# Feed-forward chunks of a decoder trunk grouped 2,2,2,1,2,2 in place of 2,2,2,2,1,2, with three groups in place of two going down in seven products

## The chip, the cores and the metric

The kernel runs on one core of one Trainium2 chip. The time is that of the device in microseconds (us) from launch to end; the lower the better. Engines are called as in the profile: PE (TensorE matmul), PEld (its weight loads), DVE (VectorE), ACT (ScalarE), SP (SyncE, which issues nearly all DMAs here), POOL (GpSimd).

## The reference

Input x is 512 tokens by 1024 channels in float32. There are two layers; each is a feed-forward block, a mixer (gated linear attention in the first layer, stick-breaking attention in the second) and another feed-forward block, all on a residual stream. So there are four feed-forward blocks, called FFN 1 to FFN 4 here:

```python
def swiglu(h, w_gate, w_up, w_down):
    return (jax.nn.silu(h @ w_gate) * (h @ w_up)) @ w_down

x = x + 0.5 * swiglu(rmsnorm(x, ffn1_norm[i]), ffn1_w_gate[i], ffn1_w_up[i], ffn1_w_down[i])
...
x = x + 0.5 * swiglu(rmsnorm(x, ffn2_norm[i]), ffn2_w_gate[i], ffn2_w_up[i], ffn2_w_down[i])
```

w_gate and w_up are 1024 by 2816, w_down is 2816 by 1024. The change touches only how these three products are cut.

## The kernel before, in words

**Number format.** Every float32 matrix is split into a high part and the remainder (names ending in h and l: `wh`, `wl` of a weight, `hh`, `hl` of the hidden activations). A product is three matmuls: high by high, low by high, high by low. The split of a loaded weight (`raw` or `rawd`) is one cast on ACT (line L527, writes `wh`) and one subtraction on DVE (line L528, writes `wl`).

**Chunks.** The 2816 hidden channels are cut into 11 chunks of 256. A chunk has a gate product, an up product (each 1024 by 256 weights), and then its 256 rows of w_down. Chunks 2 to 10 take gate and up in seven half-size products in place of eight (Strassen-Winograd, method `seven`): sums of weight quarters are made on DVE (L1082, L1083, L1088, L1089), seven products of 12 matmuls each run over 256 tokens (L1097, tiles `ps_w`, `ps_q`, `ps_z`), and results are combined on ACT and DVE. For one chunk the gate is 84 matmuls, the up 84.

**Groups and the way down.** Chunks are gathered in groups. Going down, a group of two chunks is a product of 512 hidden channels by 1024 outputs. Its usual form (function `down`) is four parts of 24 matmuls over 512 tokens, `ps_d` at L469, each with one 128x1024 weight tile to split and two additions into the residual tiles (L727). The other form (function `seven_down`) is two parts; a part loads two 512 KB blocks (`lower`, `upper`, both tagged `rawd`, of which there are two buffers in all), makes four sums on DVE (L756, L757, L763, L764), takes seven products of 12 matmuls over 256 tokens (L772) and does twelve half-size additions into the residual (L778). A group that goes down this way must close its activations differently as well (`close_first`, `close_second`): four subtractions at L1265 and more splits at L1195 for every chunk.

In the list of work a group's way down stands inside the next group: between its gates and ups. The last group's stands at the end.

**What sets the order.** The program is written as a list of entries (`feed`), and a planner in the kernel (class `Planner`) then sets the order of each engine's instructions by a list schedule with prices of its own: 148 + 1.045 n for a DVE operation of n columns, 2000 ns + bytes / 400 for a DMA. PE, DVE, ACT and SP then run in exactly that order; each waits at its own front for what the instruction there needs. Eight PSUM banks are handed out in turn; a part of `seven_down` holds five, a gate or up in seven products three. Split weights have four buffers, loaded gate and up weights two.

The lines that matter here are the tables of the class FFN and the two places where the parts of `seven_down` are put into the list:

```python
GROUPS = ((0, 2), (2, 4), (4, 6), (6, 8), (8, 9), (9, 11))
DOWN_SEVEN = (1, 3)
...
if late and i == late[0][0]:
    seven_down(*late.pop()[1])
...
if group - 1 in self.DOWN_SEVEN and i == 1:
    args = (lambda: self.tp, wd, self.GROUPS[group - 1][0] * 256, self.hs[group - 1])
    seven_down(*args, 0)
    late.append((0 if slots > 2 else 1, (*args, 1)))
```

Of the kernel before, what the change touches and what calls it, by code (L numbers as in the profile page):

```python
# [435 lines left out]
def decoder(ctx: ExitStack, tc: tile.TileContext, a: dict, out: bass.AP):  # L436
# [43 lines left out]
    class Chunk:  # L480
        def __init__(self, src, n, m):
            self.src, self.n, self.m, self.t = src, n, m, None
            self.pool = None
            self.few = False
# [95 lines left out]
    feed = Feed()  # L580

    def cols(w, c0, n):
        return w[:, c0 : c0 + n].rearrange("(k p) c -> p k c", p=P)

    def feat(ch, f, evac, tag=None, defer=None):


        def body(W):
            (wh, wl), = W
            ps = psum("ps_f", tag)  # L590
            for part in (range(u, u + KD // 4) for u in range(0, KD, KD // 4)):
                for k in part:
                    mm3(ps, wh[:, k], wl[:, k], st["h"][k], st["l"][k], k == 0, k == KD - 1)
                if part[-1] == KD - 1:
                    if defer is None:
                        evac(ps)
                    else:
                        defer.append((evac, ps))
                yield

        feed.q.append(Entry([(ch, lambda t: t[:, :, f * P : (f + 1) * P], KD, P)], body))
        feed.q[-1].evac = evac
# [97 lines left out]
    def down(w, r0, nf, hs, part, nxt, late=0):  # L700


        nd = KD // nf
        src = w[r0 : r0 + nf * P, part * nd * P : (part + 1) * nd * P]
        ch = Chunk(src.rearrange("(f p) c -> p f c", p=P), nf, nd * P)
        ch.few = True

        def body(W):
            (wh, wl), = W
            acc = []  # L710

            def prod(m, fs):
                if m == len(acc):
                    acc.append(psum("ps_d"))
                s = slice(m * P, (m + 1) * P)
                for f in fs:
                    mm3(acc[m], wh[:, f, s], wl[:, f, s], hs[f][0], hs[f][1], f == 0, f == nf - 1)

            if late:
                for m in range(nd):  # L720
                    prod(m, range(nf - late))
            for m in range(nd):
                prod(m, range(nf - late if late else 0, nf))
                ps = acc[m]
                k = part * nd + m
                x = pair(xs[k])
                nc.vector.scalar_tensor_tensor(  # L727
                    out=x, in0=flat(ps), scalar=0.5, in1=x, op0=ALU.mult, op1=ALU.add
                )
                if nxt is not None:  # L730
                    nxt(k)
                yield

        feed.q.append(Entry([(ch, lambda t: t, nf, nd * P)], body))
# [99 lines left out]
    def back_tok(w, r0, nf, hs, done):  # L834


        units = []
        for dh in range(2):
            src = w[r0 : r0 + nf * P, dh * 512 : dh * 512 + 512]
            ch = Chunk(src.rearrange("(f p) c -> p f c", p=P), nf, 512)  # L840
            for u in range(0, nf, 2):
                units.append((ch, (lambda t, u=u: t[:, u : u + 2]), 2, 512))

        def body(W):
            for i in range(NT):
                s = slice(i * P, (i + 1) * P)
                for dh in range(2):
                    cuts = (0, 256, 512) if (i, dh) == (NT - 1, 1) else (0, 512)
                    for c0, c1 in zip(cuts, cuts[1:]):
                        ps = psum("ps_bt")[:, 0 : c1 - c0]  # L850
                        c = slice(c0, c1)
                        for f in range(nf):
                            wh, wl = W[dh * (nf // 2) + f // 2]
                            hh, hl = hs[f]
                            mh, ml = turns(wh[:, f % 2, c]), turns(wl[:, f % 2, c])
                            mm(ps, hh[:, s], mh, f == 0, False)
                            mm(ps, hh[:, s], ml, False, False)
                            mm(ps, hl[:, s], mh, False, f == nf - 1)
                        done(dh, i, ps, c0, c1)
            yield  # L860

        feed.q.append(Entry(units, body))
# [132 lines left out]
    class FFN:  # L995
# [3 lines left out]

        GROUPS = ((0, 2), (2, 4), (4, 6), (6, 8), (8, 9), (9, 11))
        NORMED, SEVEN, AHEAD = 6, 2, 2
        DOWN_SEVEN = (1, 3)
        SEVEN_UP = (2, 3, 4, 5, 6, 7, 8, 9, 10)

        def __init__(self, wg, wu, wd, gi, nxt, first=False, last=False):
            self.gi, self.normed = gi, False
            self.after_ffn = bool(phases) and isinstance(phases[-1], FFN)
            self.defer, self.gates = [], []  # L1010
            self.lead = []
            self.hs = [[] for _ in self.GROUPS]
            base, downs, late = len(feed.q), [], []
            self.sums_by = 10**6
            for group, (c0, c1) in enumerate(self.GROUPS):
                slots, put = 2 * (c1 - c0), 0
                if group == 1:

                    for put in range(self.AHEAD):
                        down(*downs[put], late=put == 0)  # L1020
                    put = self.AHEAD
                for i in range(slots):
                    c, f = c0 + i // 2, i % 2
                    if f == 0:
                        g, u = Chunk(cols(wg, c * 256, 256), KD, 256), Chunk(cols(wu, c * 256, 256), KD, 256)
                    d = self.defer if i == 0 and c == 0 else None
                    f_ = f
                    if first and c == 0:

                        g, u = (Chunk(cols(w, f * P, P), KD, P) for w in (wg, wu))  # L1030
                        self.lead += [g, u]
                        f_ = 0
                    if c >= self.SEVEN:
                        if f == 0:
                            self.sums_by = min(self.sums_by, len(feed.q) - base)
                            self.seven(g)
                    elif c not in self.SEVEN_UP:
                        feat(g, f_, self.evac_g, defer=d)
                    elif f == 0:
                        feat(g, 0, self.evac_g), feat(g, 1, self.evac_g)  # L1040
                        self.sums_by = min(self.sums_by, len(feed.q) - base)
                    if c not in self.SEVEN_UP:
                        feat(u, f_, lambda ps, h=group: self.evac_u(ps, h), defer=d)
                    elif f == 1:
                        self.seven(u, group)

                    if late and i == late[0][0]:
                        seven_down(*late.pop()[1])
                    while c >= self.SEVEN and put < len(downs) * (i + 1) // slots:
                        down(*downs[put])  # L1050
                        put += 1
                    if group - 1 in self.DOWN_SEVEN and i == 1:
                        args = (lambda: self.tp, wd, self.GROUPS[group - 1][0] * 256, self.hs[group - 1])
                        seven_down(*args, 0)

                        late.append((0 if slots > 2 else 1, (*args, 1)))
                for x in downs[put:]:
                    down(*x)
                n = 2 * (c1 - c0)
                end = group + 1 == len(self.GROUPS)  # L1060
                downs = [(wd, c0 * 256, n, self.hs[group], part, nxt if end else None) for part in range(n)]
                if group in self.DOWN_SEVEN:
                    downs = []
            self.count = len(feed.q) - base
            if last:
                back_tok(wd, c0 * 256, n, self.hs[group], nxt)
            else:
                for x in downs:
                    down(*x)
            self.total = len(feed.q) - base  # L1070

        def seven(self, ch, group=None):
# [89 lines left out]
            def close_0(o0):  # L1162
                if group in self.DOWN_SEVEN:
                    self.close_first(o0, group)
                else:
                    self.close(o0, group)

            def close_1(o0, o1):
                if group in self.DOWN_SEVEN:
                    self.close_second(o0, o1, group)  # L1170
                else:
                    self.close(o1, group)
# [1116 lines left out]
```

## Time and profile before

| | us |
|---|---|
| median of 3 runs | 1762.15 |
| lowest, highest | 1761.73, 1762.88 |
| the profiled execution's own time | 1761.07 |
| its span, first to last instruction | 1759.3 |
| PE busy | 1748.0 (99%) |
| DVE busy | 1530.7 (87%) |
| ACT busy | 1055.2 (60%) |
| DMA, mean | 102 GB/s |

An engine's busy time is the time in which at least one of its instructions is running. Durations of single instructions overlap the next one's start on PE, ACT and DVE, so what an instruction costs its engine is the distance from its start to the start of the next when nothing is waited for. The granted PE clock was 0.999 over the span.

### The profile page before, as it was taken

The page shows a single profiled execution, that of the slowest core. Times are in us where ns is not written, and L with a number is a line of the kernel's source. Part 1 is how long each engine was busy: PE and PEld are TensorE (multiplying, and loading weights), DVE is VectorE, ACT ScalarE, POOL GpSimd, SP SyncE. Part 2 cuts the span into 40 slices and gives each one's busy share as a digit, 9 for nine tenths or more (in the row PEclk, how much of TensorE's full clock was granted, in tenths as well). Part 3 has the DMA queues.
Part 4 walks back from the last instruction along what each step waited for, and adds up shares of the span by engine and source line. Part 5 has one row for each costly group of instructions (what it writes and reads, how often), then busy time and mean ns, then how long its engine had stood idle before and what let it go on. Part 6 is the DMA issues. An engine that isn't in the chain of part 4 may idle for free.

```text
span 1759.3 us, 31137 instructions
## 1 busy us (share of the span) xinstructions
PE 1748.0 (99%) x12714; PEld 1631.7 (93%) x12714; DVE 1530.7 (87%) x2516; ACT 1055.2 (60%) x1830; POOL 9.9 (1%) x24
## 2 busy tenths in 40 slices
PE   9999999999999999999999999999999999999998
PEld 8999999899888899999889999999888889999997
DVE  8998898787888999988799988986898679999986
ACT  7556565545656566555556655656889755665554
POOL 0000000100000000000000000000000000000000
PEclk9999999999999999999999999999999999999999
DMA  6334323421233331432424343332222233324331
GB/s 192 120 97 133 108 73 110 142 73 50 72 96 96 120 110 60 147 117 85 148 72 129 97 131 110 108 97 72 61 73 73 72 96 120 121 68 148 97 130 50
DMA packets 178755, 179.24 MB, mean 102 GB/s; under 512 B 4082, under 2 KB 170276, under 8 KB 178612
## 3 DMA queue, kind: packets, MB, share of 16 engines
q1 hardware_dynamic: 177760, 175.91, 31.8%
q8 instruction: 99, 1.62, 0.4%
q0 software_dynamic: 608, 1.05, 0.2%
q14 instruction: 44, 0.36, 0.1%
q10 hardware_dynamic: 244, 0.29, 0.0%
HBM read 175.17 MB, written 2.10 MB: 101 GB/s over the span
## 4 chain that ended last, share of the span: by engine, by line
PE 87%; DVE 7%; DMA 2%; ACT 2%; issue 1%; SPq 0%; DVEq 0%; ACTq 0%
PE ps_w L1097 21%; PE ps_d L469 15%; PE ps_f L469 13%; PE ps_q L1097 11%; PE ps_z L1097 5%; PE ps_t L469 5%; PE ps_w L772 4%; PE ps_b L469 3%; PE ps_q L772 2%; DVE wl L528 2%; DMA raw<-in_ffn_w_gate_dram 1%; PE ps_z L1777 1%; PE ps_z L772 1%; DMA raw<-in_ffn_w_up_dram 1%; PE ps_S L469 1%
## 5 line engine op out<-in xcount | busy, mean ns | idle before, releaser
L528 DVE TENSOR_TENSOR wl<-raw,wh 128x1024 fp32r<-128x1024 f32 x241 | 254.4, 1058 | 50.1 <-ACT wh L527 49.2
L527 ACT CAST wh<-raw 128x1024 fp32r<-128x1024 f32 x241 | 221.6, 921 | 114.0 <-PE ps_f L469 26.3
L527 ACT CAST wh<-s 128x1024 fp32r<-128x1024 f32 x176 | 184.1, 1047 | 98.7 <-DVE s L1083 21.3
L1097 PE MATMUL ps_w<-th,wh 128*128 128x256 f32 x864 | 237.6, 275 | 0.0
L1097 PE MATMUL ps_w<-tl,wh 128*128 128x256 f32 x864 | 237.6, 275 | 0.0
L1097 PE MATMUL ps_w<-th,wl 128*128 128x256 f32 x864 | 237.6, 275 | 0.0
L528 DVE TENSOR_TENSOR wl<-s,wh 128x1024 fp32r<-128x1024 f32 x176 | 213.3, 1217 | 10.1 <-ACT wh L527 9.8
L469 PE MATMUL ps_f<-xh,wh 128*128 128x512 f32 x432 | 166.4, 385 | 0.0
L1097 PEld LDWEIGHTS ps_w<-th,wl 128*128 128x128 f32 x864 | 165.9, 192 | 0.0
L1097 PEld LDWEIGHTS ps_w<-th,wh 128*128 128x128 f32 x864 | 165.9, 192 | 0.0
L1097 PEld LDWEIGHTS ps_w<-tl,wh 128*128 128x128 f32 x864 | 165.9, 192 | 0.0
L469 PE MATMUL ps_f<-xh,wl 128*128 128x512 f32 x432 | 163.7, 379 | 0.0
L469 PE MATMUL ps_f<-xl,wh 128*128 128x512 f32 x432 | 163.7, 379 | 0.0
L469 PE MATMUL ps_d<-hh,wh 128*128 128x512 f32 x416 | 158.8, 382 | 0.8 <-ACT wh L527 0.7
L469 PE MATMUL ps_d<-hl,wh 128*128 128x512 f32 x416 | 157.9, 380 | 0.9 <-DVE hl L1195 0.9
L469 PE MATMUL ps_d<-hh,wl 128*128 128x512 f32 x416 | 157.7, 379 | 0.0
L527 ACT CAST wh<-rawd 128x1024 fp32r<-128x1024 f32 (+1 forms) x100 | 82.9, 846 | 73.6 <-PE ps_d L469 62.7
L528 DVE TENSOR_TENSOR wl<-rawd,wh 128x1024 fp32r<-128x1024 f32 (+1 forms) x100 | 94.9, 962 | 14.2 <-ACT wh L527 13.4
L469 PEld LDWEIGHTS ps_f<-xl,wh 128*128 128x128 f32 x432 | 81.6, 189 | 11.5
L469 PEld LDWEIGHTS ps_f<-xh,wh 128*128 128x128 f32 x432 | 81.7, 189 | 11.0
L469 PEld LDWEIGHTS ps_f<-xh,wl 128*128 128x128 f32 x432 | 81.7, 189 | 10.7
L469 PEld LDWEIGHTS ps_d<-hl,wh 128*128 128x128 f32 x416 | 78.7, 189 | 12.5 <-DVE hl L1195 1.8
(349 smaller groups left out, 5236.9 us busy)
## 6 DMA issues: line engine op xcount, KB each, us to landing
raw<-in_ffn_w_gate_dram SPq DMA_DIRECT2D x43, 1024.0 KB, 5.4
raw<-in_ffn_w_up_dram SPq DMA_DIRECT2D x43, 1024.0 KB, 5.5
rawd<-in_ffn_w_down_dram SPq DMA_DIRECT2D x84, 512.0 KB, 6.5
raw<-in_gla_w_in_dram SPq DMA_DIRECT2D x12, 1024.0 KB, 5.3
raw<-in_sb_w_in_dram SPq DMA_DIRECT2D x16, 512.0 KB, 3.7
raw<-in_gla_w_out_dram SPq DMA_DIRECT2D x4, 1024.0 KB, 5.0
raw<-in_sb_w_in_dram SPq DMA_DIRECT2D x4, 1024.0 KB, 5.0
raw<-in_sb_w_out_dram SPq DMA_DIRECT2D x4, 1024.0 KB, 5.2
```

What stands on the lines that cost most here:

```text
L469: nc.tensor.matmul(ps, l, r, start=first, stop=last)
L527: nc.scalar.copy(h[:, k], part)
L528: nc.vector.tensor_tensor(out=l[:, k], in0=part, in1=h[:, k].bitcast(F32), op=ALU.subtract)
L772: st["pe"] = nc.tensor.matmul(ps, l_, r_, start=first and c + n == 0, stop=c == 1 and n == 2, skip_group_check=True).ins
L1097: st["pe"] = nc.tensor.matmul(o, l_, r_, start=first and j + n == 0, stop=j == 3 and n == 2, skip_group_check=True).ins
L1777: nc.tensor.matmul(o_, l_, r_, start=first, stop=last, skip_group_check=True)
```

## The change

The groups become 2,2,2,1,2,2 chunks: the group of one chunk is now the fourth and not the fifth. Groups 1, 2 and 4 go down in seven products in place of groups 1 and 3 (groups are counted from 0; each of these has two chunks). Both parts of a `seven_down` now stand in the list behind the first gate of the next group and before that chunk's up; before, part 0 stood behind the first up of that group and part 1 later, behind another chunk's gate or up.

```diff
-        GROUPS = ((0, 2), (2, 4), (4, 6), (6, 8), (8, 9), (9, 11))
+        GROUPS = ((0, 2), (2, 4), (4, 6), (6, 7), (7, 9), (9, 11))
         NORMED, SEVEN, AHEAD = 6, 2, 2
-        DOWN_SEVEN = (1, 3)
+        DOWN_SEVEN = (1, 2, 4)
...
                     elif f == 0:
                         feat(g, 0, self.evac_g), feat(g, 1, self.evac_g)
                         self.sums_by = min(self.sums_by, len(feed.q) - base)
+                    if group - 1 in self.DOWN_SEVEN and f == 0 and c == c0:
+                        args = (lambda: self.tp, wd, self.GROUPS[group - 1][0] * 256, self.hs[group - 1])
+                        seven_down(*args, 0)
+                        seven_down(*args, 1)
...
-                    if late and i == late[0][0]:
-                        seven_down(*late.pop()[1])
...
-                    if group - 1 in self.DOWN_SEVEN and i == 1:
-                        args = (lambda: self.tp, wd, self.GROUPS[group - 1][0] * 256, self.hs[group - 1])
-                        seven_down(*args, 0)
-
-                        late.append((0 if slots > 2 else 1, (*args, 1)))
```

Lines behind the table move up by three (L1097 becomes L1094, L1195 becomes L1192).

The planner sets a new order. The first place is SP's queue in FFN 3, from the last usual load of group 0's way down on. `rawd` are blocks of w_down, `raw` weights of a gate or an up. Before:

```order
L494 DMA rawd_11202<-in_ffn1_w_down_dram 128x4x256
L494 DMA rawd_11308<-in_ffn1_w_down_dram 128x4x256
L494 DMA raw_11313<-in_ffn1_w_gate_dram 128x8x256
L494 DMA raw_11439<-in_ffn1_w_up_dram 128x8x256
L494 DMA raw_11575<-in_ffn1_w_gate_dram 128x8x256
L494 DMA rawd_11701<-in_ffn1_w_down_dram 128x4x256
L494 DMA rawd_11822<-in_ffn1_w_down_dram 128x4x256
L494 DMA rawd_11827<-in_ffn1_w_down_dram 128x4x256
L494 DMA raw_11883<-in_ffn1_w_up_dram 128x8x256
```

Now:

```order
L494 DMA rawd_11209<-in_ffn1_w_down_dram 128x4x256
L494 DMA raw_11283<-in_ffn1_w_gate_dram 128x8x256
L494 DMA rawd_11367<-in_ffn1_w_down_dram 128x4x256
L494 DMA rawd_11507<-in_ffn1_w_down_dram 128x4x256
L494 DMA rawd_11512<-in_ffn1_w_down_dram 128x4x256
L494 DMA rawd_11620<-in_ffn1_w_down_dram 128x4x256
L494 DMA raw_11625<-in_ffn1_w_up_dram 128x8x256
L494 DMA raw_11755<-in_ffn1_w_gate_dram 128x8x256
L494 DMA raw_11885<-in_ffn1_w_up_dram 128x8x256
```

Before, three loads of gate and up weights stood between part 0's two blocks (11202, 11308) and part 1's (11701, 11822). Now part 1's blocks (11512, 11620) follow part 0's (11367, 11507) directly; since there are two `rawd` buffers, each is issued when DVE has read the block two loads ahead of it for the last time.

The second place is DVE at the passage from part 0's preparation to part 1's in that pair, now:

```order
L528 TENSOR_TENSOR wl_11611<-rawd_11367,wh_11610 128x512
L528 TENSOR_TENSOR wl_11611<-rawd_11507,wh_11610 128x512
L1192 TENSOR_TENSOR t34_11500<-ts_11486,t34_11499 128x512
L1140 TENSOR_TENSOR o1_11549<-u3_11639,o1_11549 128x256
L1144 TENSOR_TENSOR o0_11548<-ps_q_11546,o0_11548 128x256
L528 TENSOR_TENSOR wl_11617<-s34_11542,wh_11616 128x1024
L756 TENSOR_TENSOR s12_11622<-rawd_11620 128x512
L763 TENSOR_TENSOR s34_11670<-rawd_11512,rawd_11620 128x512
L757 TENSOR_TENSOR s12_11622<-s12_11622,rawd_11512 128x512
```

The first two rows are the last readers of part 0's blocks; the row of L756 is the first of part 1's. Four DVE instructions stand between them. In the order before, 38 stood there.

More of the change, by code (lines that the diff above doesn't have):

```diff
@@ L1012, in __init__ @@
             self.hs = [[] for _ in self.GROUPS]
-            base, downs, late = len(feed.q), [], []
+            base, downs = len(feed.q), []
             self.sums_by = 10**6
```

## The prediction

> **What bounds the kernel now.** I read the page's busy table first, then the groups by line, then the chain of waits and the timeline around one pass of `seven_down`. The busy table and the biggest wait of PE in the feed-forward blocks:
>
> ```profile
> PE 1748.0 (99%) x12714; PEld 1631.7 (93%) x12714; DVE 1530.7 (87%) x2516; ACT 1055.2 (60%) x1830; POOL 9.9 (1%) x24
> L469 PE MATMUL ps_d<-hh,wh 128*128 128x512 f32 x416 | 158.8, 382 | 0.8 <-ACT wh L527 0.7
> ```
>
> PE works all the time, so its matmul time is what a change can win. DVE is second, and its 87% is a mean. By stretches it looks like this: the first row is FFN 1 from the first way down to the last up, the second the same of FFN 3, the third two gates and ups with a part of `seven_down` in FFN 3 between them.
>
> ```profile
> 52.30:305.80 253.50, 253.50 (x2065) 247.51 (x2065) 232.73 (x383) 146.08 (x257) 1.04 (x1) 1.00 0.34 107
> 917.60:1166.20 248.60, 248.49 (x2042) 242.96 (x2042) 225.86 (x372) 142.41 (x251) 0.00 (x0) 1.00 0.34 108
> 1085.43:1123.15 37.72, 37.72 (x339) 37.72 (x338) 37.24 (x64) 23.95 (x44) 0.00 (x0) 1.00 0.20 64
> ```
>
> Columns: stretch and length, then busy time (instructions) of PE, PEld, DVE, ACT, POOL, then PE clock, DMA share, GB/s. Over the body DVE is idle for about 21 of 250 us; around `seven_down` it is idle for 0.5 of 37.7 us, and PE still does not wait. So DVE may be full for a while without harm: it runs ahead of PE. How far shows in the timeline, at the start of that part:
>
> ```profile
> 1097.68 0.69 DVE L528 TENSOR_TENSOR wl<-rawd,wh 128x512 fp32r<-128x512 f32 x1
> ...
> 1104.30 0.28 PE L772 MATMUL ps_w<-nh,wl 128*128 128x256 f32 x1
> ```
>
> The weight that PE takes at 1104.30 was split by 1097.68 + 0.69 = 1098.37, a lead of 5.9 us.
>
> **The change part by part.** *PE.* One group per FFN goes from the usual form to seven products. Both rates stand in the chain of waits:
>
> ```profile
> 1051.29 5.18 PE ps_d L469 x24
> 1104.35 1.34 PE ps_w L772 x12
> ```
>
> Usual form: 4 parts of 24 matmuls are 4 x 5.18 = 20.72 us. Seven products: 2 parts x 7 x 12 matmuls are 14 x 1.34 = 18.76 us. That is -1.96 us for each FFN, -7.84 us in all.
>
> *DVE.* What an operation costs there is the distance between starts, read where nothing waits:
>
> ```profile
> 1105.91 1.21 DVE L528 TENSOR_TENSOR wl<-s,wh 128x1024 fp32r<-128x1024 f32 x1
> 1107.04 0.68 DVE L528 TENSOR_TENSOR wl<-raw,wh 128x512 fp32r<-128x512 f32 x1
> 1107.64 0.41 DVE L778 SCALAR_TENSOR_TENSOR x<-ps_q,x 128x256 f32<-128x256 f32 x1
> 1107.98 0.41 DVE L778 SCALAR_TENSOR_TENSOR x<-ps_w,x 128x256 f32<-128x256 f32 x1
> ```
>
> 1.13 us for 1024 columns (1105.91 to 1107.04), 0.60 for 512 (to 1107.64), 0.335 for 256. The usual way down: 4 splits of 1024 and 8 additions of 512, 4.5 + 4.8 = 9.3 us. `seven_down`: 8 sums of 512, splits of 6 x 512 and 4 x 1024, 24 additions of 256: 4.8 + 3.6 + 4.5 + 8.0 = 20.9 us, which is more than its 18.8 us of PE. Closing the group's activations costs 8 subtractions of 256 (2.7 us) and splits of 4 x 256 and 5 x 512 in place of 4 x 512 (4.3 against 2.4 us). So DVE gets 11.6 + 2.7 + 1.9 = 16.2 us more for each FFN while PE gets 2.0 less.
>
> Does it fit? By groups, as DVE / PE us. A gate is 7.1 / 9.4; an up 9.6 / 9.4, or 11.95 / 9.4 where the group closes for seven products; the single chunk's way down 7.1 / 10.4 (2 splits, 8 additions). Before, the groups 2 to 5 with the way down that stands in each: 54.3/56.3, 47.4/58.2, 37.6/37.5, 40.5/47.9. Now: 59.0/56.3, 37.6/37.5, 45.2/47.9, 54.3/56.3. Sums: 179.8/199.9 before, 196.1/198.0 now. DVE's free time there shrinks from 20 us to 1.9 us, but it still fits, and only the first of the four groups is now clearly over PE, by 2.7 us, less than the lead of 5.9.
>
> *Inside a pair.* The two parts now follow each other, so I count along the orders of DVE and PE in FFN 3 from the first split of part 0 (lead 5.9) to the split or addition whose product comes tightest. Pair 1 (in group 2): 19.3 us of DVE against 15.4 of PE leaves 2.0. Pair 2: 15.0 against 10.6 leaves 1.6. Pair 3: 15.7 against 10.6 leaves 0.9. None goes under zero: DVE's work alone makes no stall.
>
> *The loads.* Part 1's two blocks are loaded into the buffers of part 0 when DVE has read them for the last time. The DVE work in the order between the last reader of part 0's second block and the first reader of part 1's is 2.4, 4.35 and 3.1 us in the pairs 1, 2, 3 of each FFN, the same in all four. How long a load takes: a pair of issues, 0.6 us apart, then the time to landing (last column) of its first and its second, of a block issued alone, and the page's median:
>
> ```profile
> 1100.80 0.97 SPq L494 DMA_DIRECT2D rawd<-in_ffn_w_down_dram  x2
> ...
> rawd<-in_ffn_w_down_dram SPq DMA_DIRECT2D x1, 512.0 KB, 3.6
> ...
> rawd<-in_ffn_w_down_dram SPq DMA_DIRECT2D x1, 512.0 KB, 5.0
> ...
> rawd<-in_ffn_w_down_dram SPq DMA_DIRECT2D x1, 512.0 KB, 3.4
> ...
> rawd<-in_ffn_w_down_dram SPq DMA_DIRECT2D x84, 512.0 KB, 6.5
> ```
>
> A second block issued 0.6 us behind a first takes 5.0; one with the queue to itself 3.5. In pair 1 the two buffers come free 0.6 us apart, so I take 5.0: DVE stands for 5.0 - 2.4 = 2.6 us at L756, and behind that instruction stand the additions into the residual that PE needs before it may go on in `ps_w`; 2.6 against a margin of 2.0 is a stall of 0.6 us. In the pairs 2 and 3 they come free 1.8 us apart, so I take 3.6: no wait in pair 2, and 0.5 against 0.9 in pair 3. That is +0.6 us for each FFN, +2.4 in all. Bounds: with 3.4 everywhere nothing stalls; with the median of 6.5 everywhere it is 2.1 + 0.5 + 2.5 = 5.1 us for each FFN, +20.4 in all. The median comes from blocks queued behind 1024 KB loads of gates and ups, and here the queue in front is empty of these, so I stay near the single issues.
>
> *The PSUM banks.* A pair takes ten banks of eight. Part 1's first `ps_q` product takes the bank of part 0's second `ps_w`, whose last addition it must wait for; PE has 1.34 us of other work between. One addition is 0.41 us; behind one split of 1.21 it is 1.6. So between nothing and 0.3 us a pair; I take nothing, since the margins above already count that addition.
>
> *The end of an FFN.* The single chunk's way down no longer stands between the last up and the last group's way down, so the closing of the last chunk has less cover. It is a multiplication, a cast and a split in a row:
>
> ```profile
> L1110 DVE TENSOR_TENSOR o<-o,o 128x256 f32<-128x256 f32 x72 | 30.4, 422 | 1.8
> L1194 ACT CAST hh<-o 128x512 fp32r<-128x512 f32 x56 | 34.8, 621 | 6.0 <-DVE o L1110 5.8
> L1195 DVE TENSOR_TENSOR hl<-o,hh 128x512 fp32r<-128x512 f32 x56 | 37.4, 682 | 0.0
> ```
>
> Their means make 1.7 us, covered by the 9 matmuls that can go first, 9 x 5.18 / 24 = 1.9 us. Bounds 0 and, if DVE is as late as it allowed itself with 5.18 us more in front, some 2 us; I take 0.2 for FFN 1 to 3, +0.6; in FFN 4 the 32 transposes still stand between. In return the 0.7 us that `ps_d` waited for ACT's cast goes, since that product is moved into the block.
>
> The sum: 1761.07 - 7.84 + 2.4 + 0.6 - 0.7 = 1755.5 us in terms of the profiled execution, whose span is 1759.3. The median of the runs is 1.1 above that execution, so I forecast 1756.6 us.
>
> **The rivals.** *All of it is kept.* No load is late: 1761.07 - 7.84 - 0.7 = 1752.5, with the 1.1 1753.6 us. For it speaks that PE had next to no waits before, with DVE as full as in the third stretch; against it that DVE has 1.9 us free where it had 20.
>
> *DVE becomes the bound and the gain is given back.* DVE cannot use every nanosecond: in 1085.43:1123.15, with work at hand all the time, it is idle 1.3% of the time, in the body as a whole 8 to 9%, for want of work or behind ACT's casts. If 5% of the 196.1 us are lost to such waits, the groups 2 to 5 need 205.9 on DVE against 198.0 of PE; 5.9 of that lies in the lead at the start, and the other 2.0 us for each FFN are all that it wins: 1762 us, no change.
>
> *The loads are late in every pair.* This is the one that ends slower. Its place is DVE's front at the first sum of part 1, its price is landing time less the 2.4, 4.35 or 3.1 us of work in between, less the margin. It decides from a landing of 5.2 us in the pairs 1 and 3 (0.8 + 1.2 = 2.0 us, all that an FFN wins); at 6.5 the time is 1762.15 - 7.84 + 20.4 = 1774.7 us. Against it stands that nothing is queued in front of these blocks.
>
> *Every DVE operation costs its whole length.* Then a gate is 7.9, an up 10.95 or 13.8, the pair 24.4 and the groups 2 to 5 now 224.4 us on DVE against 198.0: about 26 - 6 = 20 us for each FFN, some 1835 us. The rows above with starts 0.60 apart at a length of 0.68 speak against it. The Trainium skill, "VectorE: DVE Perf Modes", section "The DRAIN you can't avoid", has it that the next operation does not start until the pipe is empty; by that rule the whole length would count. The trace does not agree where operations follow each other without a wait, as those four rows show.
>
> That the third group does not go down in seven products is ruled out by the order: 288 more matmuls, 72 for each FFN.
>
> **How the numbers follow.** My forecast, part of the gain given back to pair 1 and the ends, has 0.51 (1755 to 1758.6); all kept 0.16; gain given back 0.22; late loads 0.10; whole lengths 0.01. The measurement of this kernel tells no change from one of 0.2%, 3.5 us, that is from 1758.6 to 1765.7. Faster by more than that are the first two, 0.67; the third is within it, with 0.22; slower are the last two, 0.11. The range that should hold it 8 times in 10 is 1753.0 to 1763.0: from all kept to a little over no change; it leaves out the late loads and the edge of the third case.
>
> **What would show it.** In the profile after: L772 has 504 matmuls in an FFN where it had 336, and `ps_d` 96 fewer. If the steps are right, DVE's wait for `rawd` at L756 appears once in each FFN at about 2.6 us and PE waits for DVE's additions (x, L778) in pair 1 by about half a us; DVE busy in the body rises from 226 to 233 us to 242 to 249 us in a stretch 2 us shorter. If loads are late, that wait appears three times in each FFN at over 2 us and PE's at over 0.8. If DVE is the bound, its idle time in groups 2 to 5 vanishes without waits for `rawd`, and PE waits at splits (wl, L528). I am wrong if PE's total waiting in the four blocks exceeds some 6 us, or if the rate of 1.34 us for 12 matmuls does not hold.

## The result and the profile after

The changed kernel takes 1757.07 us (median, single runs from 1755.01 to 1759.72) against 1761.80 us: a ratio of 0.9973, with a 95% interval of 0.9966 to 0.9980. The forecast was 1756.6 us. The profiled execution took 1758.69 us; its span of 1756.9 is 2.4 us shorter than the 1759.3 of before, so it is one of the longer ones, and some of what follows in it is chance. A second profile of the same kernel, below, tells how much.

The busy table of the changed kernel:

```profile
PE 1743.7 (99%) x13002; PEld 1635.7 (93%) x13002; DVE 1583.9 (90%) x2688; ACT 1079.4 (61%) x1906; POOL 9.9 (1%) x24
```

PE has 288 more matmuls and is busy 4.3 us less; DVE has 172 more instructions (43 for each FFN) and is busy 53.2 us more, 13.3 for each FFN.

Now the stretch from the first to the last matmul of the gates, ups and ways down in seven products (L1097 and L772 before, L1094 and L772 now), FFN 1 to 4 in the rows, by the view of busy times in stretches (columns as in the prediction). Before:

```profile
62.50:305.68 243.18, 243.18 (x2018) 238.47 (x2017) 222.46 (x366) 141.08 (x251) 1.04 (x1) 1.00 0.35 111
...
1478.92:1723.08 244.16, 243.43 (x2019) 238.51 (x2018) 222.07 (x366) 141.79 (x250) 0.54 (x1) 1.00 0.36 115
sum 974.04, PE 973.20 PEld 953.96 DVE 886.73 ACT 565.52 POOL 1.58; mean PE 243.30 PEld 238.49 DVE 221.68 ACT 141.38 POOL 0.39
```

And of the changed kernel:

```profile
62.96:310.32 247.36, 247.31 (x2114) 244.16 (x2113) 239.41 (x413) 148.74 (x271) 1.04 (x1) 1.00 0.35 111
600.91:848.00 247.09, 247.03 (x2114) 244.01 (x2113) 238.44 (x412) 149.23 (x270) 0.00 (x0) 1.00 0.35 110
920.74:1168.39 247.65, 247.29 (x2114) 243.96 (x2113) 237.69 (x411) 148.07 (x269) 0.00 (x0) 1.00 0.34 109
1476.92:1725.92 249.00, 247.16 (x2115) 243.98 (x2114) 239.07 (x414) 149.17 (x270) 0.53 (x1) 1.00 0.35 113
sum 991.10, PE 988.78 PEld 976.11 DVE 954.61 ACT 595.21 POOL 1.58; mean PE 247.20 PEld 244.03 DVE 238.65 ACT 148.80 POOL 0.39
```

The stretch is longer, not shorter, since the last 5.18 us of the single chunk's way down now stand ahead of its end and not behind it. By the products alone each should be 5.18 - 1.96 = 3.22 us longer, 974.04 + 4 x 3.22 = 986.9 in all, and some 0.7 less for the stall that FFN 4 had before. It is 991.1. So about 4.2 to 4.9 of the 7.8 us were lost again inside these four stretches, about half of that in FFN 4. Of this loss 2.3 us is idle time of PE (991.10 - 988.78); the rest the profile counts as busy, so the rows of PE's waits below do not add up to all of it. Outside the four stretches the changed kernel loses 1.3 us more: 1756.9 - 991.10 = 765.8 us, where 1759.3 - 974.04 - 4 x 5.18 = 764.5 would be left.

Where? The waits of DVE that are new (total, how often, longest, in us):

```profile
DVE s L756 <- DMA rawd<-in_ffn_w_down_dram: 8.8, 8, 2.7
```

And the waits of PE at the ways down, in the same columns:

```profile
PE ps_w L772 <- DVE x L778: 1.8, 2, 1.5
PE ps_d L469 <- DVE hl L1192: 1.4, 2, 1.0
...
PE ps_q L772 <- DVE x L778: 0.2, 1, 0.2
```

DVE waits at the first sum of a part for its block of w_down, 8 times where it never did before, and PE waits for the additions into the residual that are queued on DVE behind that sum. Of these three waits of PE two are in pair 1 of FFN 4 (1.5 and 0.3 us) and one of 0.2 us in pair 3 of FFN 3; none is in the other pairs. (The row of `ps_d` lies ahead of FFN 2 and FFN 4, where nothing was changed; it was 0.9 us before, and more on that follows.) The worst place is pair 1 of FFN 4. In the chain of waits:

```profile
1531.24 0.03 DVE t L1192
1531.27 6.76 DMA rawd<-in_ffn_w_down_dram
1538.03 0.02 issue
1538.05 0.69 DVE s L756
...
1540.55 1.33 DVE x L778 x4
```

and in the timeline of PE, with the idle time ahead of the instruction in brackets:

```profile
1541.27 0.38 PE L772 MATMUL ps_w<-nh,wh 128*128 128x256 f32 x1 [1.52 <-DVE x L778]
```

From the timeline, for part 1's second block in each pair, this is how long the load took from its issue (landing) and how long DVE waited for it:

| pair, FFN 1 / 2 / 3 / 4 | landing, us | DVE's wait at L756, us |
|---|---|---|
| 1 (behind group 1) | 4.5 / 4.5 / 4.4 / 6.8 | 0.6 / 0.4 / 0.4 / 2.7 |
| 2 (behind group 2) | 4.2 / 3.9 / 4.3 / 4.0 | 0 / 0 / 0 / 0 |
| 3 (behind group 4) | 4.4 / 4.3 / 5.0 / 4.4 | 1.0 / 1.0 / 1.6 / 1.0 |

### The profile page after: what moved, and what is told of

Its sections match the earlier page's. It is cut to its first block, busy times and chain, and to the rows that moved or that the text cites. A ratio compares the mean times of both kernels' runs of the same rounds, so it can differ in the third digit from the quotient of the medians.

```text
span 1756.9 us, 32000 instructions
## 1 busy us (share of the span) xinstructions
PE 1743.7 (99%) x13002; PEld 1635.7 (93%) x13002; DVE 1583.9 (90%) x2688; ACT 1079.4 (61%) x1906; POOL 9.9 (1%) x24
## 4 chain that ended last, share of the span: by engine, by line
PE 78%; DVE 15%; DMA 2%; ACT 2%; issue 2%; DVEq 0%; ACTq 0%; SPq 0%
PE ps_w L1094 17%; PE ps_f L469 14%; PE ps_d L469 9%; PE ps_q L1094 9%; PE ps_w L772 5%; DVE wl L528 5%; PE ps_t L469 5%; PE ps_z L1094 4%; PE ps_b L469 4%; PE ps_q L772 3%; DVE x L778 2%; PE ps_z L1774 1%; PE ps_z L772 1%; DMA rawd<-in_ffn_w_down_dram 1%; PE ps_S L469 1%
## 5 line engine op out<-in xcount | busy, mean ns | idle before, releaser
L527 ACT CAST wh<-s 128x1024 fp32r<-128x1024 f32 x192 | 201.6, 1051 | 141.2 <-DVE s L1080 38.3
L1094 PE MATMUL ps_w<-th,wh 128*128 128x256 f32 x864 | 238.3, 276 | 0.0
L528 DVE TENSOR_TENSOR wl<-s,wh 128x1024 fp32r<-128x1024 f32 x192 | 234.4, 1222 | 3.7 <-ACT wh L527 3.7
L1094 PE MATMUL ps_w<-th,wl 128*128 128x256 f32 x864 | 237.6, 275 | 0.0
L1094 PE MATMUL ps_w<-tl,wh 128*128 128x256 f32 x864 | 237.6, 275 | 0.0
L1094 PEld LDWEIGHTS ps_w<-th,wh 128*128 128x128 f32 x864 | 165.8, 192 | 0.3
L1094 PEld LDWEIGHTS ps_w<-tl,wh 128*128 128x128 f32 x864 | 165.9, 192 | 0.0
L1094 PEld LDWEIGHTS ps_w<-th,wl 128*128 128x128 f32 x864 | 165.9, 192 | 0.0
L469 PE MATMUL ps_d<-hl,wh 128*128 128x512 f32 x288 | 109.4, 380 | 1.4 <-DVE hl L1192 1.4
L469 PE MATMUL ps_d<-hh,wh 128*128 128x512 f32 x288 | 109.8, 381 | 0.4 <-ACT hh L1191 0.2
L469 PE MATMUL ps_d<-hh,wl 128*128 128x512 f32 x288 | 109.2, 379 | 0.0
L527 ACT CAST wh<-rawd 128x512 fp32r<-128x512 f32 (+1 forms) x108 | 80.7, 766 | 20.9 <-PE ps_d L469 12.0
L528 DVE TENSOR_TENSOR wl<-rawd,wh 128x512 fp32r<-128x512 f32 (+1 forms) x108 | 92.9, 866 | 0.3 <-ACT wh L527 0.3
L1094 PE MATMUL ps_q<-th,wh 128*128 128x256 f32 x288 | 79.3, 275 | 0.0
```

What stands on the lines that cost most here:

```text
L469: nc.tensor.matmul(ps, l, r, start=first, stop=last)
L527: nc.scalar.copy(h[:, k], part)
L528: nc.vector.tensor_tensor(out=l[:, k], in0=part, in1=h[:, k].bitcast(F32), op=ALU.subtract)
L1094: st["pe"] = nc.tensor.matmul(o, l_, r_, start=first and j + n == 0, stop=j == 3 and n == 2, skip_group_check=True).ins
```

## The experiments

Ratios are to the kernel before, which ran beside each.

**The same kernel again: how much of FFN 4 is chance.** No edit.

> The changed kernel once more, for a second profile. The first one showed DVE waiting for a block of w_down at L756 in the first and the third pair of each FFN (0.4 to 0.6 us in pair 1 of FFN 1 to 3, 2.7 us in FFN 4, 1.0 to 1.6 us in pair 3), and PE waiting 2.2 us in pair 1 of FFN 4. If the long landing there (6.8 us) is chance, pair 1 of FFN 4 shows 0.4 to 0.6 us now like the others and PE next to nothing, and PE's waiting in the four bodies falls from 4.1 to about 2 us; if something always collides there, the 2.7 us are back. Time 1757 either way, single runs up to 2.5 us apart.

1757.14 us, 0.9973 (0.9963 to 0.9983). The same four stretches in its profile, summed:

```profile
sum 988.69, PE 988.19 PEld 975.94 DVE 954.53 ACT 595.27 POOL 1.58; mean PE 247.05 PEld 243.98 DVE 238.63 ACT 148.82 POOL 0.39
```

Its waits of DVE at L756:

```profile
DVE s L756 <- DMA rawd<-in_ffn_w_down_dram: 6.1, 8, 1.2
```

The waits of DVE stand at the same eight places. Pair 1 of FFN 4 is again the worst, but with a landing of 5.3 us, a wait of 1.2, and PE starts late by 0.2 and 0.5 us there. So the extra time in FFN 4 is partly chance (its stretch is 2.3 us over the products' 246.7 in one profile, 0.7 in the other), partly not: that block lands late in both. The four stretches sum to 988.7, 1.8 us over the products' 986.9 instead of 4.2; outside them 1.6 us are lost (1754.8 - 988.69 = 766.1 against 764.5). What is lost in a usual execution lies near these: this profile was taken of an execution of 1756.54 us, 0.6 under the median.

**What makes the block land late: loads behind it?** In the changed kernel two loads of 1024 KB follow part 1's blocks in SP's queue at once; here they stand ahead of them and are issued when their own buffers come free.

```diff
+                        ahead = Chunk(cols(wg, (c + 1) * 256, 256), KD, 256)
+                        feed.q[-2].pre += [(u,), (ahead,)]
...
-                for u in e.units:
+                for u in [*e.pre, *e.units]:
                     u[0].load()
```

> The loads of the next up and the next gate (1024 KB each) stand in SP's queue ahead of part 1's blocks and not right behind them. Theory of the loads: part 1's second block takes 4.4 to 5.0 us (once 6.8) because two 1024 KB loads are issued within 1.0 us behind it and share the DMA engines; alone it takes 3.5 us. DVE's waiting at L756 then falls from 8.8 to 1 or 2 us, PE's in the bodies from 4.1 to 1 us or less, and the time to about 1754.5 us. Rival, DVE is full: the waits at L756 go, others take their place, PE waits as long, 1757 us. Rival, the landing is the block's own price (second in the queue): 4.4 us as before, 1757 us.

1756.39 us, 0.9968 (0.9957 to 0.9980), not to be told from the run above. PE, DVE and ACT run the same order as in the changed kernel; only SP's differs. SP's timeline ahead of pair 1 of FFN 1 (the last row is part 1's two blocks):

```profile
98.93 0.71 SPq L494 DMA_DIRECT2D raw<-in_ffn_w_up_dram  x1
106.84 0.37 SPq L494 DMA_DIRECT2D raw<-in_ffn_w_gate_dram  x1
116.46 0.97 SPq L494 DMA_DIRECT2D rawd<-in_ffn_w_down_dram  x2
```

The second of the two by the view of DMA issues, whose last column is the time to landing:

```profile
rawd<-in_ffn_w_down_dram SPq DMA_DIRECT2D x1, 512.0 KB, 4.5
```

The big loads are issued 10 and 18 us ahead, and the second block still takes 4.5 us. DVE's waits at L756 are as before:

```profile
DVE s L756 <- DMA rawd<-in_ffn_w_down_dram: 6.8, 8, 1.3
```

So the theory that the loads behind the block make it late fell; the second rival, the price of a block that is second in the queue, is what remains. The Trainium skill, "DMA: Bandwidth & Descriptors", section "Queues, rings and completion order", says that each DMA engine consumes its descriptors in ring order; by that rule loads behind a block should not delay it, and this pair of runs agrees: 4.49 us with them right behind, 4.45 without.

**The place and the buffer, apart.** `place_only` has the groups of before (two in seven products) with both parts behind the next gate:

```diff
-        GROUPS = ((0, 2), (2, 4), (4, 6), (6, 7), (7, 9), (9, 11))
+        GROUPS = ((0, 2), (2, 4), (4, 6), (6, 8), (8, 9), (9, 11))
...
-        DOWN_SEVEN = (1, 2, 4)
+        DOWN_SEVEN = (1, 3)
```

The third buffer takes its 4 KB for each partition from the temporaries, so four of these are run alone too:

```diff
-                    self.t = st["few"].tile([P, self.n, self.m], F32, tag="rawd", bufs=2, name="rawd")
+                    self.t = st["few"].tile([P, self.n, self.m], F32, tag="rawd", bufs=3, name="rawd")
...
-                name="tp", bufs=5, reuse_waits="tile"
+                name="tp", bufs=4, reuse_waits="tile"
```

`place_only`, two buffers:

> The groups of before (2,2,2,2,1,2, two of them in seven products), but both parts behind the next chunk's gate. PE's products are those of before, so this shows what the place alone costs. Theory of the loads: two pairs for each FFN, each with a DVE wait of 0.4 to 1.6 us at L756 and PE stalls of 0 to 0.8 us: 1762 to 1764 us. Rival, the place costs nothing: 1761.8 us. Rival, the place itself is a gain (the parts no longer cut into an up): below 1761 us.

`rawd_three`, the change with the third buffer:

> A third buffer for the blocks of w_down (its 4 KB for each partition come from the temporaries, four buffers in place of five; the next run has that alone). Part 1's first block can then be loaded while part 0 is prepared, the second behind the release of part 0's first, 0.6 to 1.8 us earlier and with the queue to itself (3.5 in place of 4.4 us). Theory of the loads: DVE's wait at L756 falls from 6 to 9 us to 1 us or less, PE's in the bodies from 1.7 to 3.8 us to below 1, time 1754 to 1755 us, 2 to 3 below the next run. Rival, DVE is full: other waits, the time of the next run.

`temporaries_four`, the change with four temporaries alone:

> The changed kernel with four buffers for the temporaries in place of five, the base for the run with three buffers for w_down. No theory needs a fifth buffer in the bodies: 1757 us, DVE's waits at L756 as in the changed kernel. If temporaries are tight, up to 1 or 2 us more.

`place_rawd_three`, `place_only` with the third buffer:

> The groups of before, both parts behind the next gate, with the third buffer (four for temporaries). place_only cost 2.7 us on the kernel before. Theory of the loads: that was the waiting for part 1's blocks; with the third buffer 1761 to 1762 us. Rival, the place costs by itself (PE's order, the PSUM banks): 1764 us as without the buffer.

`before_rawd_three`, the kernel before with the third buffer:

> The kernel before with the third buffer (four for temporaries). Before, no part waited for its blocks, so theory of the loads: no change, 1761 to 1762 us. Rival, the third buffer helps by itself, whatever the placing (usual ways down, starts of an FFN): 1758 to 1759 us, as it did on the changed kernel.

| | two buffers, us | three buffers, us |
|---|---|---|
| before | 1761.5 to 1761.8 | 1761.11, 0.9992 (0.9982 to 1.0001) |
| place only | 1764.41, 1.0014 (1.0005 to 1.0023) | 1759.98, 0.9990 (0.9981 to 0.9999) |
| the change | 1757.14; with four temporaries 1756.44, 0.9969 (0.9958 to 0.9981) | 1753.50, 0.9953 (0.9940 to 0.9965) |

The third buffer is worth nothing that can be told where the parts stand apart (0.4 us), 4.4 us where two pairs stand together (4.2 by the ratios) and 2.9 us where three do, against four temporaries alone. DVE's waits at L756 in the change with four temporaries, and with the third buffer:

```profile
DVE s L756 <- DMA rawd<-in_ffn_w_down_dram: 7.0, 8, 1.7
...
DVE s L756 <- DMA rawd<-in_ffn_w_down_dram: 2.4, 3, 0.8
```

The four stretches with the third buffer, summed:

```profile
sum 986.72, PE 986.72 PEld 975.49 DVE 956.11 ACT 601.45 POOL 2.49; mean PE 246.68 PEld 243.87 DVE 239.03 ACT 150.36 POOL 0.62
```

Part 1's second block in pair 1 of FFN 1, by the view of DMA issues:

```profile
rawd<-in_ffn_w_down_dram SPq DMA_DIRECT2D x1, 512.0 KB, 3.7
```

No other block is in flight ahead of it now. The four stretches sum to 986.7, the length that the products alone give, and PE's busy time is their whole length. On the change, then, the theory of the loads holds: less waiting at L756, a shorter landing, and the loss inside the stretches gone, while the buffer does nothing for the kernel before, where no block was late. One thing came with the buffer and was not separated from it: against the run with four temporaries, the planner set 234 of DVE's 2688 instructions at other places (PE's products and SP's loads keep their order). This version beats both kernels.

For `place_only` the theory is not shown. Its median went 4.4 us down, below the 1761 to 1762 expected, but in the two profiles DVE waits as long at L756 without the third buffer as with it:

```profile
DVE s L756 <- DMA rawd<-in_ffn_w_down_dram: 4.0, 8, 0.6
...
DVE s L756 <- DMA rawd<-in_ffn_w_down_dram: 4.1, 5, 0.9
```

The profiled execution of `place_only` was its shortest (1762.42), and its four stretches are 0.8 us longer than before (974.86 against 974.04); the further 2 us of its median are in executions that were not profiled. What the buffer takes away there stays open.

Read by rows, the place costs 2.7 us with two buffers; with three it gains some 1.1, which the intervals do not tell from nothing. The third group in seven products with the new grouping gains 6.5 to 7.3.

**The parts where they stood before, with three groups.** The groups and `DOWN_SEVEN` of the change, put into the kernel before; for the second of the two runs this line too:

```diff
-                        late.append((0 if slots > 2 else 1, (*args, 1)))
+                        late.append((2 if c1 == 11 else 0 if slots > 2 else 1, (*args, 1)))
```

> The new groups with three of them in seven products, but the parts where they stood before: part 0 behind the first up of the next group, part 1 later. PE's products are those of the change. Theory of the loads: part 1's blocks have long landed, no wait at L756, so 7.8 us less than before are all kept: 1754 us. Rival, DVE is full: it has the same work as in the change, so about 1757 us or more.

This run is without the line above, and part 1 of the last pair is never put in: 1716.94 us with four parts missing says nothing, as 4 x 9.4 us are simply absent.

> As three_late, which lost part 1 of group 4's way down in every FFN (four parts of 9.4 us were not computed, so its time says nothing); now all parts are there. The new groups, three in seven products, part 0 behind the first up of the next group, part 1 later. Same products on PE as in the change. Theory of the loads: the blocks of part 1 are loaded long before, no wait at L756, and the 7.8 us are kept: about 1754 us. Rival, DVE is full: the work is the same, so 1757 us or more, with PE waiting elsewhere.

1753.46 us, 0.9953 (0.9941 to 0.9966). This kernel changes the values: by the code, two of a closed group's sums (`t34`) have one buffer, and the next group's overwrite them before the late part 1 has read them. So it is no version to use, and one that kept the values might have to wait where this one does not. But the numbers of products, loads and DVE operations are those of the change:

```profile
PE 1739.3 (99%) x13002; PEld 1633.8 (93%) x13002; DVE 1585.3 (91%) x2688; ACT 1086.0 (62%) x1906; POOL 9.9 (1%) x24
```

DVE never waits at L756 there, and the 7.8 us are kept, with as much work on DVE. `rawd_three` has the same 2688 DVE operations at 1753.50 us and keeps the values. So the amount of DVE's work alone does not account for the 1757 us.

**How full DVE is.** The second sum of a gate is done twice in chunks 4 to 10, unknown to the planner's prices: 28 operations, 16.8 us at 0.60.

```diff
-                nc.vector.tensor_tensor(out=s[:, 4:8], in0=s[:, 0:4], in1=t[:, 0:4, 0:P], op=ALU.subtract)
+                for k in range(1 + ch.twice): i = nc.vector.tensor_tensor(out=s[:, 4:8], in0=s[:, 0:4], in1=t[:, 0:4, 0:P], op=ALU.subtract).ins; k and FREE.add(i.name)
```

`dve_more`, on the changed kernel:

> The changed kernel with more work for DVE that changes nothing of the result: the second sum of a gate (L1080, 0.60 us) is done twice in the seven chunks 4 to 10, 4.2 us more for each FFN, all in groups 2 to 5, where the prediction left DVE 1.9 us free of 198.0. The planner does not price it. Rival, DVE is full: all beyond 1.9 us reaches PE, 2.3 us for each FFN, +9 us: 1766 us. Theory of the loads with DVE's lead of some 6 us at each pair intact: 0 to 1 us for each FFN, 1757 to 1761 us.

`before_dve_more`, on the kernel before:

> The kernel before with the same extra work for DVE (L1080 twice in the gates of chunks 4 to 10, 4.2 us for each FFN). In the changed kernel these 16.8 us cost 16.5: theory now is that the 1.9 us that DVE had free were already eaten by 1.5 to 2.2 us of waiting for blocks of w_down in each FFN. Before, 20 us were free and no load was late: 0 to 2 us in all, 1761.5 to 1763.5. Rival, the extra work hurts wherever it stands since the planner does not price it (an instruction ahead of what PE needs next, 0.6 us each time): 5 us or more, 1767 to 1778.

`rawd_three_dve_more`, on the change with the third buffer:

> Third buffer for blocks of w_down (four for temporaries), with the extra 4.2 us of DVE work for each FFN. If free time and load waits draw on one account, the waits that the third buffer took away (some 1.5 us for each FFN) pay for a part of it: 4.2 - 1.9 = 2.3 us for each FFN reach PE, +9 on the 1753.5 of the third buffer alone: 1762 to 1764 us. Rival, the extra work reaches PE whole whatever the loads do: +16.5, 1770 us.

| with 16.8 us more on DVE | time, us | more than without | for each FFN, of 4.2 |
|---|---|---|---|
| before | 1766.01, 1.0026 (1.0016 to 1.0035) | 4.5 | 1.1 |
| the change | 1773.68, 1.0071 (1.0057 to 1.0084) | 16.5 | 4.1 |
| the change, third buffer | 1766.33, 1.0022 (1.0013 to 1.0031) | 12.8 | 3.2 |

None of the three came out as expected. (Taken by the distances to the kernel before that ran beside each, 12.2 and -4.6 us, the second row is 16.8; the intervals leave some 3 us either way.) In the changed kernel about all of it reaches PE. It does so at a new place: PE waits in gates and ups for the combining of their products, which comes late on DVE and ACT. The waits of PE with the extra work, in the changed kernel:

```profile
PE ps_w L1094 <- ACT o L1127: 8.1, 9, 1.2
...
PE ps_w L772 <- DVE x L778: 1.5, 3, 1.1
```

So the changed kernel has next to no free DVE time left in groups 2 to 5; with the third buffer it has about 4.2 - 3.2 = 1.0 us for each FFN, where the prediction counted 1.9. And before, 20 us free in the groups did not make 4.2 us free of charge: 1.1 were paid. Where, the traces tell by the starts of the same matmul in both. In FFN 3 it is 0.5 us at each of these two, and 0.3 us in small steps between:

```profile
1013.90 0.38 PE L1097 MATMUL ps_w<-th,wh 128*128 128x256 f32 x1 [0.31 <-ACT ps_z L1124]
...
1161.69 0.48 PE L469 MATMUL ps_d<-hh,wh 128*128 128x512 f32 x1 [0.58 <-ACT wh L527]
```

The stretch around `seven_down` in which DVE was idle for 0.5 of 37.7 us (1085 to 1123) lies between them, so it is not where most of the price is paid.

## Why the prediction came out right, point by point

*PE's products: right.* L772 has 2016 matmuls, 504 in an FFN, and `ps_d` 384 fewer, 96 in an FFN. -7.84 us: the third buffer keeps them whole, at 1753.50, where "all of it is kept" was put at 1753.6. The rate of 1.34 us for 12 matmuls holds in the chain of the changed kernel. Last gate and way down of FFN 3 there:

```profile
1158.09 1.90 ACT wh L527 x2
1159.99 0.04 issue
1160.04 0.48 PE ps_d L469
1160.52 1.34 PE ps_q L1094 x12
```

*The end of an FFN: right size, another reason.* These rows show it: `ps_d` waits for ACT's cast of the weight, not for the split of the last activations. PE's start is late by 0.21 to 0.23 us in FFN 1 to 3 against 0.2 that I took; in FFN 3 it was late by 0.27 at its end before too, so two of the three are new. The 0.7 us in FFN 4 are gone as forecast.

*DVE's work: right in number.* 43 more operations for each FFN, as counted. They were priced at 16.2 us by distances between starts; the busy time rose by 13.3. An operation behind which DVE stands idle counts there with its whole length (0.68 us and not 0.60), and in the traces 387 of them do where it was 493; as an estimate that is 106 x 0.08 / 4 = 2.1 of the 2.9 us between.

*The loads: right place, wrong terms, and a sum that came near partly by luck.* "DVE stands for 5.0 - 2.4 = 2.6 us at L756" in pair 1 was 0.4 to 0.6 in three FFNs. The 5.0 was 4.4 to 4.5, but the larger mistake is the 2.4: I counted the work of DVE between the release of a buffer and the first sum of part 1, and not its waits. The timeline of the changed kernel in pair 1 of FFN 1:

```profile
117.44 0.69 DVE L1192 TENSOR_TENSOR t<-ts,t 128x512 fp32r<-128x512 f32 x1
118.28 0.42 DVE L1140 TENSOR_TENSOR o<-u,o 128x256 f32<-128x256 f32 x1 [0.16 <-ACT u L1139]
119.16 0.42 DVE L1144 TENSOR_TENSOR o<-ps_q,o 128x256 f32<-128x256 f32 x1 [0.46 <-PE ps_q L1094]
120.24 1.23 DVE L528 TENSOR_TENSOR wl<-s,wh 128x1024 fp32r<-128x1024 f32 x1 [0.66 <-ACT wh L527]
122.06 0.69 DVE L756 TENSOR_TENSOR s<-rawd 128x512 f32<-128x512 f32 x1 [0.59 <-DMA rawd<-in_ffn_w_down_dram]
```

The second block is issued at 117.55. DVE waits 0.16 + 0.46 + 0.66 = 1.3 us for products of the gate just running and for a cast, and these waits cover the load as well as work does. In pair 3 I took 3.6 us, the landing of a block by itself, since it is issued 1.8 us behind the first; it took 4.3 to 5.0, and DVE waited 1.0 to 1.6 us where I expected 0.5. So pair 1 was priced too high and pair 3 too low: 12.4 us of waiting by my count (4 x 2.6 and 4 x 0.5), 8.8 and 6.1 in the two profiles. The stall of PE that I put at 0.6 us in pair 1 of each FFN shows in FFN 4 alone: there PE starts 2.2 us late in the first profile and 0.7 in the second, and not over 0.2 late in pair 1 of the others. The cost to PE was put at 2.4 us; the third buffer gives 2.9 back. That the two are near is luck as far as the terms go: they were too large in one place, too small in another, and about half of the first profile's loss in the stretches comes from a single late block.

*The sum.* Of 7.84 us, 4.7 arrived by the medians (1761.80 to 1757.07); I had 5.5. The interval of the ratio reaches from 3.5 to 6.0 us, so the 0.8 between needs no cause of its own. What the prediction left out is the loss outside the stretches, 1.3 and 1.6 us in the two profiles. 1.0 and 1.1 of it stand between FFN 3's last product and FFN 4's first, in an order that the change left as it was: 308.53 and 308.59 us against 1478.92 - 1166.24 - 5.18 = 307.50. In both profiles ACT waits 2.8 us there for an up's weights, where it waited 1.6 before, and the waits of PE at `ps_d` just ahead of FFN 4 are 1.2 and 1.3 us, where they were 0.5. In `raws_first` ACT waits 1.7 us there, and the passage takes 307.51. Why that load lands later in the changed kernel is open.

*The rivals.* Loads late in every pair needed a landing of 5.2 us; it was 4.4 in most. DVE as the bound was wrong as the cause of what was lost, since the same work runs in 1753.50 us, but nearer than its 0.22 looked: its condition, next to no free time left, is met. Whole lengths: the extra operations are 683 ns long (the median of L1080 in `dve_more`), and all 100 of that line have the next operation start 0.60 to 0.61 us behind their own start. So 0.60 and not 0.68 is the price, as the prediction's rows had it; the 16.5 us alone would not tell 28 x 0.60 = 16.8 from 28 x 0.683 = 19.1. The rule quoted from the Trainium skill ("VectorE: DVE Perf Modes", "The DRAIN you can't avoid") is not what this stream of operations shows; the same section goes on that a next operation that is not held starts earlier, and with that the trace agrees. The PSUM banks: no stall of PE shows at their place that the additions behind the late sum don't explain; they were not tested by themselves.

## What to carry to other kernels

When two pieces of work are moved together, look at what they share: with two buffers, the second piece's load starts only when the first has been read, and the pair loses its lead. One more buffer was worth 2.9 us here, where loading other weights earlier was worth nothing that can be told, and it was worth nothing where the pieces stood apart. A wait for a load has to be priced with the engine's waits in that stretch, and not with its work alone. And a free share of an engine, worked out over a long stretch, is a bound and no reserve: DVE had 20 us in 200 free before, and a quarter of 4.2 us more work still reached PE.

## What the runs showed of the hardware

The second of two 512 KB loads lands 4.2 to 4.5 us after its issue in most pairs, whether it is issued 0.6 or 1.8 us behind the first (4.49 and 4.43 in FFN 1), and whether or not 2 MB are queued right behind it; where a third buffer let it be issued with no block in flight ahead of it, it took 3.4 to 3.7. In pair 1 of FFN 4 it took 6.8, 5.3 and 5.3 us in the first three profiles of the changed order, at most 5.0 elsewhere in them. Why there is not settled.
